# A hybrid decoder layer on one core: four tiles and one norm change place

## The chip, the cores and the metric

The kernel runs on one core of one Trainium2 chip. A core has five engines that run their own instruction queues in order: TensorE (PE) multiplies matrices out of SBUF into PSUM, VectorE (DVE) and ScalarE (ACT) do elementwise work, GpSimd (POOL) does a little of it here, and SyncE (SP) only issues transfers. A transfer is handed to a queue and carried by 16 DMA engines. The metric is the device time of one execution in microseconds (us); of several executions the median counts, and less is better.

## The reference

One decoder layer works on 2048 tokens of 1024 channels in float32.

```
h    = rmsnorm(x, g_mix) * (1 + sc_m) + sh_m
q, k, v, f_logit, u = split(h @ w_in)
attn = rmsnorm(forgetting_attention(q, k, v, log_sigmoid(f_logit + b)), g_attn_out)
ssm  = rmsnorm(s5_ssm(u, ...), g_ssm_out)
x    = x + gt_m * (concat(attn, ssm) @ w_out)
h    = rmsnorm(x, g_ffn) * (1 + sc_f) + sh_f
gate, val = split(h @ w_up)
x    = x + gt_f * ((silu(conv3(gate)) * val) @ w_down)
out  = rmsnorm(x, g_final)
```

The six vectors sh_m, sc_m, gt_m, sh_f, sc_f, gt_f are `silu(c) @ w_ada + b_ada`. The attention has 8 heads of 64; the state space model (ssm) has 32 groups; the middle width of the MLP is 2816 (22 tiles of 128 channels). The last line divides each token by its root mean square, so it needs all 1024 channels of a token before it can scale one of them.

## The kernel before, in words

The tokens are four blocks of 512. Nearly every product is made of three matmuls, because each operand is split into a rounded part and a rest (`_hi` and `_lo`): hi x hi, hi x lo, lo x hi. A weight goes through `w_raw` (two buffers, loaded on SP's queue), ACT makes `w_hi` from it (L77, or L107 where the rest is kept in HBM), and DVE makes `w_lo` (L78). `w_hi` and `w_lo` have three buffers each.

The program is written with tile pools, and a scheduler turns it into one fixed order for each engine, from priorities and from its own estimate of when a tile's memory comes free. Engines then wait for each other by semaphores, but never change that order. The tile pools are stacked: when a pool is closed, the next one is laid over its memory. Pools opened by the helper `opened` ask for their waits tile by tile.

The stages, in the order of time:

1. Projections of all blocks, tables of the ssm, then the ssm itself (pools `ssm` in SBUF and `ssm_ps` in PSUM) beside attention of block 0 (`attention((0,))`) and the q/k/v projections of blocks 2 and 3 (`proj_qkv`, L428, results in `vst`). In the same stage `ada_mid` (L1091) works out gt_f (`mod["tf"]`): per half, eight slices of w_ada arrive in two tiles `wada` (tags `ka3` and `ka4` of the pool `att`), DVE adds them into one accumulator `ada_mid` (L1100, L1102), and PE turns it into a column (`ada_col`, L316). The accumulator lies in the pool `ssm`. Attention holds augmented keys in the tiles `ka0` to `ka2`, taken in a cycle by the heads of block 0; after this stage `ka3`, `ka4` and `kx0` join the cycle, each after a memset on POOL (L1136).
2. The pools `ssm` and `ssm_ps` are closed; over them come `rows`, `ffn` and `act` in SBUF and the PSUM pools `ffn_ps` (three banks `ff_ps`) and `sc_ps`. `mix_t(0)` loads attention and ssm rows of block 0 (L1199, L1200), normalises them, transposes them on PE (L1212) and splits them; `out_proj(0)` multiplies by w_out (L1238); `h2_of` makes the MLP's input. These stand under high priority.
3. `attention((1, 2, 3))` is traced next at normal priority, and its matmuls (L943, L986, L987, L1007, L1011) are spread over the MLP of blocks 0 and 1, which is made in four groups of 6, 6, 5 and 5 channel tiles (`FFG`): `up` (L1264) for each tile of the group, then `down` (L1296 to L1298) for eight output tiles d, added into the tiles `yt`. In the last group of block 0 the next block's `out_proj(1)` and its norm `modulate` (L391, L379, L380) are put in. `finish(0, sq)` then makes the final norm of block 0: `token_sums` on PE (L341), `rsqrt_mean` as a chain of 12 small DVE instructions (L166 to L176), four transposes (L347), a copy on ACT (L367), eight products on DVE (L1311) and eight stores (L1313). It is traced ahead of block 1's `up`.
4. Blocks 2 and 3 share their up product in a Strassen-like form: `up_pair` makes seven products of 12 matmuls (L1387) for each of the 22 tiles. Its first two operands, b11 and b21, lie in tiles of the pool `h` (nine `h_hi`, nine `h_lo`). The results `ah` and `al` go to HBM (L1431).
5. All pools but a few are closed, `h` among them, and a pool `act` is laid over everything. `down_pair(2)` and `down_pair(3)` read the activations back (L1448, 22 tiles of 512 KB) and make the down product (L1480 to L1482): two halves of four d, four PSUM tiles `acc_ps`, the groups one after the other. In the very last group of block 3 (`cut`) each matmul is made for 256 tokens at a time, p = 0 then p = 1, so that `finish_last` (L341, L166 to L176, L347, L1517, L1521 to L1526) can norm and store the first half ahead of the second. The four weights of that group come out of the three buffers `w_hi` and `w_lo`.

Of the kernel before, what the change touches and what calls it, by code (L numbers as in the profile page):

```python
# [12 lines left out]
F32 = mybir.dt.float32  # L13
F32R = mybir.dt.float32r
# [8 lines left out]
P = 128  # L23
# [4 lines left out]
TB = S // NB  # L28
# [83 lines left out]
def hybrid_layer(ctx, tc, x, c_t, w_ada, b_col, gains, w_flat, bf_row, a_re, a_im, log_dt,  # L112
# [978 lines left out]
    def ada_mid(pool, sec, key):  # L1091

        for hf in range(2):
            acc = pool.tile([P, TB], F32, name="ada_mid", tag="ada_mid", bufs=1)
            for k in range(KT):
# [42 lines left out]

    qa_t, ka_all = itertools.cycle(aug_tiles(att_pool, "qa", 2)), aug_tiles(att_pool, "ka", 3)
    ka_t = [itertools.cycle(ka_all)]  # L1140
    att_ps = opened(att_ctx, "att_ps", bufs=1, space=PSUM, side="right")
    with tc.tile_pool(name="ssm", bufs=2) as sp, tc.tile_pool(name="ssm_ps", bufs=1, space=PSUM) as sps:
# [3 lines left out]
        attention((0,))  # L1146
        mid = itertools.chain(*(ada_mid(sp, sec, key) for sec, key in ((5, 'tf'),)))
        for b in (2, 3):
# [20 lines left out]
    yt = []  # L1169
    ka_t.append(itertools.cycle(ka_all + aug_tiles(att_pool, "ka", 2, 3) + aug_tiles(fp, "kx", 1)))  # L1170

# [262 lines left out]
    def down_pair(b, ap, dps, misc, tail):  # L1434
# [9 lines left out]
        def load_act(g):  # L1444
            c0 = sum(FFG[:g])
            for c in range(c0, c0 + FFG[g]):
                t = ap.tile([P, 2, TB], F32R, name="act", tag="act", bufs=NFF)
                Q.dma_start(t.bitcast(F32), act_d[c][b % 2])  # L1448
                act.append(t)

        load_act(0)
        for half in range(2):
# [3 lines left out]
            for g, n in enumerate(FFG):  # L1456
# [9 lines left out]
                for p in range(2 if cut else 1):  # L1466
                    ts = slice(p * 256, (p + 1) * 256) if cut else slice(0, TB)
                    for d in ds:
                        if d not in ws:
                            ws[d] = weights.get(*dn_slots[g][d])  # L1470
                        wh, wl = ws[d]
# [3 lines left out]
                        for c in range(n):  # L1475
                            ah, al = act[c0 + c][:, 0, ts], act[c0 + c][:, 1, ts]
                            a, bb = wh[:, c * P : (c + 1) * P], wl[:, c * P : (c + 1) * P]
# [87 lines left out]
    for b in range(2):  # L1565
        i = 0
        for g, n in enumerate(FFG):
            act = [up(h2, i + c) for c in range(n)]
            i += n
# [24 lines left out]
        if b == 0:  # L1594
            x1 = x1n
            finish(b, sq)
    first = up_pair(0, ops, ups)
# [34 lines left out]


# [78 lines left out]
```

## Time and profile before

| | us |
|---|---|
| median of 3 executions | 2672.63 (2672.21 to 2674.73) |
| the profiled execution | 2669.64 |
| its span | 2667.8 |
| TensorE busy in it | 2571.5 (96%) |
| mean granted TensorE clock | 0.973 |

The profiled execution lasted 2669.64 us, of which the span, from the first to the last instruction, is 2667.8; 1.84 us lie around it. It is 2.99 us below the median. A view by windows gives, for a stretch, its length and then the busy time of each engine with the number of its instructions, the clock that the throttle granted TensorE (1.00 is full speed), the share of the DMA engines' time that was busy, and the rate. A timeline gives start and length in us, the engine, the line of the kernel, and in brackets how long the engine had been idle and what released it. SPq is the issue of a transfer on SyncE's queue, not the transfer. Where matmuls follow each other closely their shown durations overlap, since they are pipelined; their spacing is what they cost.

### The profile page before, as it was taken

To read this page: it belongs to the slowest core of one execution; us is meant where nothing else is said; L and a number is where in the kernel's file an instruction comes from. 1 tells how busy PE (TensorE), PEld (TensorE's weight loads), DVE (VectorE), ACT (ScalarE), POOL (GpSimd) and SP (SyncE) were. 2 spreads that over 40 slices of the span, in tenths; PEclk is the share of its full clock that TensorE was granted. 3 is DMA by queue.
4 is the path that set the end of the run, shared out by engine and by line. 5 is a ranking of instruction groups with operands and counts; after the bars stand their busy time and mean duration, and the time that the engine had idled before them with its cause. 6 is when DMAs were issued, how large, how long until landed. Compare 5 with 4: busy or idle time off the path is not lost. (4 is left out here: it accounts for less than half of the span.)

```text
span 2667.8 us, 35631 instructions
## 1 busy us (share of the span) xinstructions
PE 2571.5 (96%) x12343; PEld 2082.7 (78%) x12343; DVE 1928.8 (72%) x3568; ACT 1240.3 (46%) x2056; POOL 190.4 (7%) x146
## 2 busy tenths in 40 slices
PE   6999999998999999999999999999979999999997
PEld 3889878886788888887788888887858888877886
DVE  7989589967787787887976867655687777762333
ACT  3423255644455545565565645555544444442221
POOL 0001000000000000000000000000043343310000
PEclk8999999998899999999899999999989999999998
DMA  8487986666456555656556555557522323236562
GB/s 316 146 268 222 306 252 202 211 205 209 148 199 224 188 183 171 201 173 204 186 181 203 190 174 194 163 203 262 189 103 97 124 97 121 98 136 239 200 225 93
DMA packets 264196, 500.62 MB, mean 188 GB/s; under 512 B 26928, under 2 KB 111792, under 8 KB 264016
## 3 DMA queue, kind: packets, MB, share of 16 engines
q1 hardware_dynamic: 262192, 493.10, 56.2%
q0 software_dynamic: 1280, 4.20, 0.4%
q8 instruction: 98, 1.61, 0.2%
q10 hardware_dynamic: 544, 1.05, 0.1%
q14 instruction: 82, 0.67, 0.1%
HBM read 371.17 MB, written 127.01 MB: 187 GB/s over the span
## 5 line engine op out<-in xcount | busy, mean ns | idle before, releaser
L78 DVE TENSOR_TENSOR w_lo<-w_raw,w_hi 128x1024 fp32r<-128x1024 f32 (+2 forms) x219 | 235.9, 1079 | 214.6 <-ACT w_hi L77 210.9
L77 ACT CAST w_hi<-w_raw 128x1024 fp32r<-128x1024 f32 (+2 forms) x219 | 203.3, 929 | 363.6 <-PE acc_ps L1481 100.9
L1264 PE MATMUL ff_ps<-h_lo,w_hi 128*128 128x512 f32 x704 | 279.3, 397 | 0.2 <-DVE h_lo L380 0.2
L1264 PE MATMUL ff_ps<-h_hi,w_lo 128*128 128x512 f32 x704 | 279.3, 397 | 0.0
L1264 PE MATMUL ff_ps<-h_hi,w_hi 128*128 128x512 f32 x704 | 279.2, 398 | 0.0
L996 ACT ACTIVATE pf<-sc_ps 128x512 f32<-128x512 f32 (+1 forms) x320 | 168.6, 542 | 165.3 <-PE sc_ps L987 84.6
L948 DVE TENSOR_REDUCE mx<-sc_ps 128x1 f32<-128x512 f32 (+2 forms) x320 | 195.8, 621 | 68.2 <-PE sc_ps L943 38.6
L998 DVE TENSOR_TENSOR pl<-pf,ph 128x512 fp32r<-128x512 f32 (+1 forms) x320 | 195.9, 620 | 29.5 <-ACT ph L997 28.8
L997 ACT CAST ph<-pf 128x512 fp32r<-128x512 f32 (+1 forms) x320 | 178.1, 568 | 81.7 <-PE o_ps L1007 78.4
L1006 DVE TENSOR_TENSOR acc<-acc,pf 128x512 f32<-128x512 f32 (+2 forms) x264 | 159.3, 606 | 22.6 <-ACT pf L996 19.4
L107 ACT CAST w_hi<-w_raw 128x1024 fp32r<-128x1024 f32 (+2 forms) x100 | 96.3, 963 | 142.9 <-PE ff_ps L1264 52.7
L1264 PEld LDWEIGHTS ff_ps<-h_lo,w_hi 128*128 128x128 f32 x704 | 132.9, 189 | 29.5 <-DVE h_lo L380 0.5
L1264 PEld LDWEIGHTS ff_ps<-h_hi,w_hi 128*128 128x128 f32 x704 | 133.1, 189 | 28.6
L1264 PEld LDWEIGHTS ff_ps<-h_hi,w_lo 128*128 128x128 f32 x704 | 132.9, 189 | 28.8
L1480 PE MATMUL acc_ps<-act,w_hi 128*128 128x512 f32 (+1 forms) x372 | 144.5, 389 | 10.6 <-DMA act<-act 6.5
L1481 PE MATMUL acc_ps<-act,w_hi 128*128 128x512 f32 (+1 forms) x372 | 143.9, 387 | 0.0
L1482 PE MATMUL acc_ps<-act,w_lo 128*128 128x512 f32 (+1 forms) x372 | 143.4, 387 | 0.2 <-DVE w_lo L78 0.2
L1296 PE MATMUL ff_ps<-act_hi,w_hi 128*128 128x512 f32 x352 | 140.0, 398 | 0.9 <-ACT rt L367 0.9
L1297 PE MATMUL ff_ps<-act_lo,w_hi 128*128 128x512 f32 x352 | 139.4, 397 | 0.0
L1298 PE MATMUL ff_ps<-act_hi,w_lo 128*128 128x512 f32 x352 | 139.0, 396 | 0.0
L986 PE MATMUL sc_ps<-qb,kb 128*128 128x512 f32 (+2 forms) x320 | 127.8, 400 | 2.3 <-DVE mx L948 1.3
L1007 PE MATMUL o_ps<-ph,vv 128*128 128x512 f32 (+1 forms) x320 | 122.2, 382 | 0.0
(521 smaller groups left out, 6457.5 us busy)
## 6 DMA issues: line engine op xcount, KB each, us to landing
w_raw<-in_w_flat SPq DMA_DIRECT2D x193, 512.0 KB
w_lo<-wlo SPq DMA_DIRECT2D x68, 512.0 KB
wlo<-w_lo SPq DMA_DIRECT2D x52, 512.0 KB
w_raw<-in_w_flat SPq DMA_DIRECT2D x64, 384.0 KB
act<-act SPq DMA_DIRECT2D x44, 512.0 KB
kb<-kb SPq DMA_DIRECT2D x80, 256.0 KB
vv<-v SPq DMA_DIRECT2D x80, 256.0 KB
w_raw<-in_w_flat SPq DMA_DIRECT2D x64, 320.0 KB
```

The costliest lines, as they stand in the source:

```text
L77: nc.scalar.copy(hi[:, :n], raw[:, :n])
L78: nc.vector.tensor_tensor(out=lo[:, :n], in0=raw[:, :n], in1=hi[:, :n].bitcast(F32), op=ALU.subtract)
L948: V.reduce_max(out=mx[:, s, ch : ch + 1], in_=ps[:, 0:n], axis=AX.X)
L996: A.activation(pf[:, cs], ps[:, cs], AF.Exp)
L997: A.copy(ph[:, cs], pf[:, cs])
L998: V.tensor_tensor(out=pl[:, cs], in0=pf[:, cs], in1=ph[:, cs].bitcast(F32), op=ALU.subtract)
L1006: eng.tensor_tensor(out=acc[j][:, cs], in0=acc[j][:, cs], in1=pf[:, cs], op=ALU.add)
L1264: T.matmul(ps, lhsT=lt, rhs=rt, start=(n == 0), stop=(n == 23))
L1296: T.matmul(ps, lhsT=a, rhs=ah[:, ts], start=(c == 0), stop=False)
L1480: T.matmul(pss[d][:, ts], lhsT=a, rhs=ah, start=st, stop=False, skip_group_check=cut)
L1481: T.matmul(pss[d][:, ts], lhsT=a, rhs=al, start=False, stop=False, skip_group_check=cut)
L1482: T.matmul(pss[d][:, ts], lhsT=bb, rhs=ah, start=False, stop=sp_, skip_group_check=cut)
```

## The change

The accumulator of `ada_mid` leaves the pool `ssm` and takes the tag `ka2` of the pool `att`; so attention of block 0 has two key tiles in its cycle (`ka0`, `ka1`), and `ka2` joins later, with `ka3`, `ka4` and `kx0`. The final norm of block 0 is traced inside block 1's first group, after the third of its six `up`. The activations of the first down group of blocks 2 and 3 are read into `h_hi` and `h_lo` (two loads of 256 KB each instead of one of 512 KB), and the pool `h` stays open to the end; the others get a tag of their own. The four weights of the last group are split into tiles of their own (`cut_hi4` to `cut_lo7`).

```diff
     def ada_mid(pool, sec, key):
-            acc = pool.tile([P, TB], F32, name="ada_mid", tag="ada_mid", bufs=1)
+            acc = pool.tile([P, TB], F32, name="ada_mid", tag="ka2", bufs=1)
...
-    qa_t, ka_all = itertools.cycle(aug_tiles(att_pool, "qa", 2)), aug_tiles(att_pool, "ka", 3)
+    qa_t, ka_all = itertools.cycle(aug_tiles(att_pool, "qa", 2)), aug_tiles(att_pool, "ka", 2)
...
-        mid = itertools.chain(*(ada_mid(sp, sec, key) for sec, key in ((5, 'tf'),)))
+        mid = itertools.chain(*(ada_mid(att_pool, sec, key) for sec, key in ((5, 'tf'),)))
...
-    ka_t.append(itertools.cycle(ka_all + aug_tiles(att_pool, "ka", 2, 3) + aug_tiles(fp, "kx", 1)))
+    ka_t.append(itertools.cycle(ka_all + aug_tiles(att_pool, "ka", 3, 2) + aug_tiles(fp, "kx", 1)))
...
         def load_act(g):
-                t = ap.tile([P, 2, TB], F32R, name="act", tag="act", bufs=NFF)
-                Q.dma_start(t.bitcast(F32), act_d[c][b % 2])
-                act.append(t)
+                if g == 0:
+                    act.append(h_parts())
+                    for j, t in enumerate(act[-1]):
+                        Q.dma_start(t.bitcast(F32), act_d[c][b % 2, :, j])
+                else:
+                    t = ap.tile([P, 2, TB], F32R, name="act", tag=f"act{c}", bufs=1)
+                    Q.dma_start(t.bitcast(F32), act_d[c][b % 2])
+                    act.append((t[:, 0], t[:, 1]))
...
                         if d not in ws:
-                            ws[d] = weights.get(*dn_slots[g][d])
+                            so, sn = dn_slots[g][d]
+                            own = [ap.tile([P, sn], F32R, name=f"w_{nm}", tag=f"cut_{nm}{d}", bufs=1)
+                                   for nm in ("hi", "lo")] if cut else (None, None)
+                            ws[d] = weights.split(weights.raw(so, sn), sn, *own)
...
-            act = [up(h2, i + c) for c in range(n)]
+            act = []
+            for c in range(n):
+                act.append(up(h2, i + c))
+                if b == 1 and g == 0 and c == 2:
+                    finish(0, sq0)
...
         if b == 0:
-            x1 = x1n
-            finish(b, sq)
+            x1, sq0 = x1n, sq
...
-    hp_ctx.close()
     with ExitStack() as stk:
...
             down_pair(b, ap, dps, misc, b == 3)
+    hp_ctx.close()
```

More of the change, by code (lines that the diff above doesn't have):

```diff
@@ L1475, in down_pair @@
                         for c in range(n):
-                            ah, al = act[c0 + c][:, 0, ts], act[c0 + c][:, 1, ts]
+                            ah, al = (t[:, ts] for t in act[c0 + c])
                             a, bb = wh[:, c * P : (c + 1) * P], wl[:, c * P : (c + 1) * P]
```

## The prediction

> **What bounds the kernel now.** I read the busy times of the page first, then windows over the whole span, and then the timelines of the engines around each window in which TensorE is short of its length or its clock is below 1.00.
>
> ```profile
> PE 2571.5 (96%) x12343; PEld 2082.7 (78%) x12343; DVE 1928.8 (72%) x3568; ACT 1240.3 (46%) x2056; POOL 190.4 (7%) x146
> ```
>
> ```profile
> 604.00:616.00 12.00, 7.90 (x45) 6.67 (x43) 7.32 (x12) 3.10 (x5) 0.54 (x2) 0.82 0.78 269
> 616.00:636.00 20.00, 15.96 (x52) 11.18 (x53) 13.85 (x45) 7.55 (x18) 0.96 (x2) 0.51 0.64 211
> 636.00:644.00 8.00, 6.28 (x38) 4.72 (x36) 7.85 (x20) 6.47 (x13) 0.00 (x0) 1.00 0.41 131
> 650.00:1250.00 600.00, 598.26 (x2743) 478.47 (x2742) 479.63 (x857) 318.66 (x530) 0.00 (x0) 0.99 0.58 191
> 1279.00:1291.00 12.00, 10.53 (x30) 5.84 (x29) 10.10 (x23) 4.38 (x9) 0.00 (x0) 0.72 0.48 146
> 1306.00:1312.00 6.00, 3.16 (x23) 2.77 (x22) 5.97 (x11) 3.76 (x6) 0.00 (x0) 0.95 0.93 327
> 1312.00:1322.00 10.00, 8.99 (x33) 7.05 (x34) 7.86 (x25) 4.32 (x9) 0.00 (x0) 0.52 0.09 33
> 1322.00:1900.00 578.00, 576.64 (x2608) 465.66 (x2607) 391.06 (x731) 316.04 (x520) 0.00 (x0) 1.00 0.60 200
> ```
>
> TensorE bounds it: 598.26 of 600 us and 576.64 of 578 us in the long stages. So a microsecond that TensorE gets back ahead of such a stage ends the program a microsecond earlier, as long as the same instructions remain. There are two ways to lose one: idle time, and work at a clock of about one half, which follows a place where TensorE had idled. I price the second as busy time x (1 - clock). The change touches four such places.
>
> **Place 1, the accumulator (604 to 644).** Idle time is 4.10 + 4.04 + 1.72 us; the clock costs 7.90 x 0.18 = 1.4 and 15.96 x 0.49 = 7.8. Together 19.1 us are lost here. The instructions around it:
>
> ```profile
> 589.74 0.32 SPq L1044 DMA_DIRECT2D att<-at  x1
> ...
> 617.71 0.33 SPq L1199 DMA_DIRECT2D row<-att  x1
> ```
>
> ```profile
> 616.45 0.52 POOL L1136 MEMSET kx<- 3x512 f32 x1
> ```
>
> ```profile
> 615.98 1.87 PE L316 MATMUL sc_ps<-ones,ada_mid 128*128 128x1 f32 x8 [1.62 <-DVE ada_mid L1102]
> ...
> 628.21 0.80 PE L987 MATMUL sc_ps<-qa,ka 67*128 67x512 f32 x1 [3.82 <-DMA qa<-rrow]
> ...
> 635.99 0.82 PE L1212 MATMUL ff_ps<-ident,row 128*128 128x128 f32 x6
> ...
> 642.46 0.47 PE L1238 MATMUL ff_ps<-yt,w_hi 128*128 128x512 f32 x1
> ```
>
> ```profile
> 614.84 0.42 DVE L489 TENSOR_TENSOR vst<-vq_ps,vst 128x256 fp32r<-128x256 f32 x1
> ```
>
> ```profile
> 592.00:600.00 8.00, 8.00 (x69) 7.91 (x68) 4.59 (x8) 2.91 (x5) 0.00 (x0) 1.00 0.46 157
> ```
>
> The last attention tile of block 0 is stored at 589.74, but its rows are fetched only at 617.71, though `mix_t(0)` has high priority; and kx0, which needs no data, is set at 616.45. Both lie over the memory of the pool `ssm`, and both come with the last reader of `ada_mid` (L316, 615.98). I read this as the scheduler holding the whole pool for that one tile. With the accumulator in `ka2`, the row loads may go at about 592, and squares, rsqrt and scaling follow on ACT and DVE. The next wait is then for PSUM: the `ff_ps` banks lie where `vq_ps` was, whose last reader is the DVE instruction that ends at 615.26. From first transpose to first `out_proj` matmul took 642.46 - 635.99 = 6.5 us, so `out_proj(0)` can start at 621.7 instead of 642.46, and it is 192 matmuls that need no attention result of block 1. They cover the wait of 3.82 for `rrow` and the 1.72 idle after 636: 5.5 us. Of the 15.96 us busy, 5.6 lie ahead of 621.7; the other 10.4 x 0.49 = 5.1 come back but for about 0.7 while the clock recovers: 4.4. Against it stand eight row loads of 256 KB, 2.1 MB, ahead of v stores, weights and `wada` in SP's queue. At the rate of the twelve 512 KB loads quoted under place 3 (6.29 MB in 17.04 us, 369 GB/s) they are 5.7 us of transfer, and 592 to 600 has 8 x 0.54 = 4.3 free. So the v projection is late by 1.4 to 2 us. The other edits here I cost at nothing: with two key tiles in block 0 a head's key load waits for the head before last, as its `qa` load (two tiles) does already; `ka2` is set only after L316, with its load some 5 us later than before, and the second head's maxima that need it give way to `out_proj`. If that cover is gone, it costs those 5. **I take 8.0 us**; bounds -5.7 (all transfer time lands on TensorE, nothing is filled) and 19.1.
>
> **Place 2, the norm of block 0 (1306 to 1322).** Idle 2.84 + 1.01; the clock 8.99 x 0.48 + 3.16 x 0.05 = 4.5; together 8.3 us.
>
> ```profile
> 1306.10 0.39 PE L1298 MATMUL ff_ps<-act_hi,w_lo 128*128 128x512 f32 x1
> ...
> 1309.78 0.66 PE L1042 MATMUL sc_ps<-ident,sums 128*128 128x128 f32 x4 [2.51 <-ACT sums L1039]
> ...
> 1320.25 1.06 PE L347 MATMUL ff_ps<-ident,rs_y 128*128 128x128 f32 x4
> ...
> 1320.96 0.77 PE L1264 MATMUL ff_ps<-h_hi,w_hi 128*128 128x512 f32 x1
> ```
>
> ```profile
> 1302.01 1.42 DVE L380 SCALAR_TENSOR_TENSOR h_lo<-h_f,mod_sf,h_hi 128x512 fp32r<-128x512 f32 x2
> ...
> 1313.85 0.76 DVE L380 SCALAR_TENSOR_TENSOR h_lo<-h_f,mod_sf,h_hi 128x512 fp32r<-128x512 f32 x1
> ...
> 1322.49 5.38 DVE L1311 SCALAR_TENSOR_TENSOR yt<-yt,gain,rt 128x512 f32<-128x512 f32 x8
> ```
>
> The last down matmul of block 0 is at 1306.10, and block 1's `up` begins at 1320.96, right behind the norm's transposes, though four of its eight input tiles are ready by 1303.4 and the last at 1314.6. Without the norm in front, 4 tiles x 3 matmuls x 2 branches = 24 matmuls can run at once; at 576.64 / 2608 = 0.22 us each they last 5.3 us, to 1311.6, by when tiles arrive in twos. The gap of 2.51 is filled, and with it goes the half clock. DVE is busy 5.97 of 6.00 us there, so the late tiles may still be waited for; that is why I keep back 1.8. The norm itself (12 small matmuls, a chain of 12 DVE instructions, the 5.38 us on DVE, eight stores of 256 KB) comes some 30 us later among three further `up`, which are its cover, and ends ahead of the first down that writes `yt`. It holds an `ff_ps` bank twice. If the transposes stand too near to their sums, TensorE waits for the chain, 3.10 us by a row of place 4. **I take 6.5 us**; bounds -3.1 and 8.3.
>
> A rule of the Trainium skill ("TensorE: Matmul & The Clock Gate", section "Part 1: The HAM clock gate (the "warmup" mystery)") says that the clock halves after an idle window of about 3.4 us and returns after about 3.4 us of sustained work. By it the 2.51 us here would not have been enough to halve the clock, and filling it need not bring the clock back; the row of 1312 to 1322 has 0.52 behind it all the same.
>
> **Place 3, from up to down (2387 to 2431).**
>
> ```profile
> 2373.14 0.39 PE L1387 MATMUL up_y<-h_hi,w_lo 128*128 128x512 f32 x1
> ...
> 2393.96 0.76 PE L1480 MATMUL acc_ps<-act,w_hi 128*128 128x512 f32 x1 [6.48 <-DMA act<-act]
> ```
>
> ```profile
> 2380.78 8.68 SPq L69 DMA_DIRECT2D w_raw<-in_w_flat  x3
> 2389.50 17.04 SPq L1448 DMA_DIRECT2D act<-act  x12
> ```
>
> ```profile
> 2371.00:2387.00 16.00, 16.00 (x70) 12.93 (x69) 9.02 (x12) 6.03 (x9) 0.00 (x0) 1.00 0.35 116
> ...
> 2394.00:2397.00 3.00, 3.00 (x8) 2.38 (x9) 1.22 (x1) 1.04 (x1) 0.00 (x0) 0.54 0.90 333
> ...
> 2425.00:2431.00 6.00, 6.00 (x15) 4.35 (x15) 2.37 (x3) 1.34 (x2) 0.00 (x0) 0.51 0.72 218
> ```
>
> ```profile
> PE acc_ps L1480 <- ACT w_hi L77: 3.6, 1, 3.6
> ```
>
> ```profile
> 2396.33 7.76 DMA act<-al
> ```
>
> TensorE waits 6.48 us for the first activation, whose load is issued at 2389.50, when the pools are closed. In the `h` tiles it need not wait for that: b11 and b21 are read for the last time at 2373.14, and up to 2387 the DMA engines are 65% free, 10 us, while 3.1 MB take 8.5. So the first down matmul follows the last up matmul: 6.48 + 3.00 x 0.46 = 7.9 us. A second wait, 3.6 us for a weight queued behind the activations, with 6.00 x 0.49 = 2.9 of clock, I leave as it is: 3.1 MB less are in the queue, but TensorE also comes 6.5 us sooner. If it goes too, the gain is 14.4. The other way: the next group's tiles lie over `rows`, which the store of `al` leaves only at 2404.1, and a load took 4.5 us from 2389.50 to its matmul, so 2408.6; four d of 18 matmuls at 0.22 us end at 2403.4. That would be a new wait of 5.2 with 2.9 of clock, -0.2 in all. The store's 7.76 us stand behind twelve loads that will be gone, so **I take 7.9 us**, by the row of the 6.48 us wait; bounds -0.2 and 14.4. Block 3's loads into `h` are covered by a full TensorE.
>
> **Place 4, the end.**
>
> ```profile
> 2650.70 0.50 PE L341 MATMUL misc_ps<-ones,sq_acc 128*128 128x1 f32 x4
> 2654.30 0.45 PE L347 MATMUL misc_ps<-ident,rs_y 128*128 128x128 f32 x1 [3.10 <-DVE rs_y L176]
> ...
> 2660.11 0.66 PE L347 MATMUL misc_ps<-ident,rs_y 128*128 128x128 f32 x2 [4.40 <-DVE rs_y L176]
> ```
>
> ```profile
> 2642.74 0.73 ACT L77 CAST w_hi<-w_raw 128x640 fp32r<-128x640 f32 x1 [0.20 <-PE acc_ps L1481]
> ```
>
> ```profile
> 2651.90 0.42 DVE L333 TENSOR_TENSOR sq_acc<-sq_acc,sq 128x256 f32<-128x256 f32 x1
> ...
> 2661.29 2.05 DVE L1524 SCALAR_TENSOR_TENSOR yt<-yt,gain,misc_ps 128x256 f32<-128x256 f32 x5 [1.33 <-ACT rt L1517]
> ```
>
> The fourth weight is split at 2642.74, when a buffer is released by the first weight's second half; so the first half's sums come at 2650.70, after all 120 matmuls, and the second half's norm queues behind the first's on PE (3.10) and on DVE (4.40). With four buffers of its own the first half is complete after 60 of the 120 matmuls, and its norm runs beside the other 60. The second half's squares are ready at 2651.90 + 0.42 = 2652.3, as now. Sums of 0.50 and an undisturbed chain of 3.10 give 2655.9; then, as now, 2661.29 - 2660.11 = 1.2 to the first product, so 2657.1 instead of 2661.29. **I take 4.2 us**; bounds 1 (the two chains still meet on DVE) and 6 (the squares are earlier too, by the waits that the present order puts between the matmuls).
>
> **Sum.** 8.0 + 6.5 + 7.9 + 4.2 = 26.6 us. The profiled execution took 2669.64, so 2643.0; it lies 2.99 below the median 2672.63, and the sum carried to the median is 2646.0.
>
> **The rivals.** (A) Place 1 pays nothing: `opened` asks for waits by tile, so something else may order the rows, or transfers and `rrow` take the place of the wait: 2654.0. For it speaks a DMA share of 0.78 from 604 to 616. (B) Place 3's wait turns up one group later, as worked out: 2654.1. (C) The waits that I left go too, 13.6 (the two later windows of place 1), 8.3, 14.4 and 6 us: 2630.3. (D) The idle time of place 2 goes but the half clock has another cause and stays, 4.5 us: 2650.5; the page named above speaks for it, the row of 0.52 against it. (E) The change does not do what it says: the scheduler's order stays the same in the first three places and only the end pays: 2668.4, no change that can be measured. (F) Slower: the new order loses the cover elsewhere. From 1279 to 1291 attention's DVE work already starves TensorE, 1.47 idle and 10.53 x 0.28 = 2.9 of clock, 4.4 us. Blocks 1 to 3 have 24 heads; from seven more such places the gain is gone, and at eight more the time is 2646.0 + 35.2 = 2681.2. Against it: in 1200 us of that stage this is the one large place.
>
> **How the numbers follow.** The forecast has 0.42, A 0.17, B 0.12, C 0.08, D 0.08, E 0.07, F 0.06. A difference below 0.2%, 5.3 us, is about what a measurement of this kernel cannot tell from none. So faster 0.87, same 0.07 (E), slower 0.06 (F). The range goes from C, 2630, to 2663, where A and B come together (2662.1); it leaves out E and F, 0.13, and some of the edges. The likeliest time is 2646.0.
>
> **What would show it.** Place 1: `row<-att` issued near 593, and L1238 beginning near 622. Place 2: L1264 of block 1 right behind the last L1298, and the clock at 1.00 through it. Place 3: no wait of L1480 for `act`, its loads ahead of the last up matmul. Place 4: L77 of the last weight ahead of the first L341, and the wait of 4.40 of the last L347 about as short as the 3.10 of the one before. I would be wrong if TensorE's idle time moved to another window instead of leaving, above all next to transfers at 590 to 610 and 2400 to 2425.

## The result, and the profile after

The changed kernel takes 2659.72 us (median of 4 executions, 2654.97 to 2661.21) against 2673.24 us for the kernel before on the same chip (4 executions, 2672.21 to 2674.73). The ratio is 0.9946, with a 95% interval of 0.9929 to 0.9963: 13.5 us less, between 10 and 19. Repeated later it was 2657.83 us, ratio 0.9944 (0.9932 to 0.9956). The forecast was 2646.0, a gain of 26.6 us. The time lies inside the range of 2630 to 2663, the sign was right, and about half of the gain was there.

To see where it went, I counted TensorE's lost time: in rows of 5 us of the view by windows, (5 - busy) + busy x (1 - clock), summed over each stretch. This is the pricing of the prediction, applied to the whole span. One column is one profiled execution; the kernels of the later columns are explained under the experiments.

```
us lost              before norm   h    cut   no    acc  | after again load load  mix  late load  all
                            alone alone alone acc   alone|                  +tail            +late
0 to 575              55.5  57.9  59.7  59.8  62.8  59.6 | 62.7  59.3  57.4  60.4  55.7  56.8  57.1  59.3
575 to 725 (place 1)  27.2  26.0  27.9  26.8  24.8  22.9 | 19.7  22.1  21.0  20.4  19.3  14.0  17.1  16.6
725 to 1225            0.0   0.2   0.2   0.1   0.5   0.0 |  0.0   0.0   0.0   0.0   0.0   0.9   0.9   0.5
1225 to 1400 (pl. 2)  13.2   8.2  13.1  14.0   7.0  17.8 |  6.5   6.2   4.8  11.3   6.3   8.1   9.0  10.9
  of it 1225 to 1275   0.0   0.0   0.0   0.0   0.0   0.0 |  1.7   0.0   0.0   0.0   0.0   4.0   5.5   5.3
  of it 1275 to 1300   4.7   4.8   4.4   4.3   3.4  10.7 |  0.0   0.0   0.0   0.0   0.0   0.0   0.0   0.0
  of it 1300 to 1400   8.5   3.4   8.7   9.7   3.6   7.1 |  4.8   6.2   4.8  11.3   6.2   4.1   3.6   5.6
1775 to 1850           1.4   1.4   1.4   1.4   1.4   1.2 |  0.1   0.1   0.6   0.1   0.1   0.1   0.1   0.2
1850 to 1990          19.5  20.2  20.0  20.6  20.6  18.0 | 24.5  23.3  24.2  22.1  23.1  22.6  25.2  23.1
2350 to 2600 (pl. 3)  14.7  15.4   8.6  15.2   8.0  13.9 |  9.2   8.6   4.1   2.8   8.7   9.5   4.4   3.1
2600 to the end (4)   16.2  15.5  16.1  13.0  13.2  15.6 | 13.5  13.3  13.0  13.7  13.5  13.6  13.5  13.6
```

(Nothing is lost between 1400 and 1775 and between 1990 and 2350 in any of them. The span less the lost time is 2520.0 in the profile before and 2519.2 to 2525.4 in the others, so the count closes within about 6 us and not better.)

The first row is no effect of the change. The kernels "norm", "h", "cut" and "no acc" have, up to 575 us, the same order of instructions on PE, DVE, ACT and SP as the kernel before, and still read 57.9 to 62.8; the kernel before reads 55.5. The kernels with the order of the change read 55.7 to 62.7 there. So the 7.2 us between the profile before and the profile after are no more than what chance gives; the profile before happens to be the lowest of all. The places have to be read one by one.

**Place 1.** The timeline of the kernel after, SP's queue and then PE:

```profile
575.97 0.54 SPq L1199 DMA_DIRECT2D row<-att  x1
...
588.26 0.47 SPq L934 DMA_DIRECT2D kx<-kb  x1
...
613.82 0.32 SPq L1044 DMA_DIRECT2D att<-at  x1
615.92 0.32 SPq L1199 DMA_DIRECT2D row<-att  x1
```

```profile
619.37 3.54 PE L1212 MATMUL ff_ps<-ident,row 128*128 128x128 f32 x16 [1.04 <-DVE vst L489]
628.16 1.09 PE L347 MATMUL ff_ps<-ident,rs_y 128*128 128x128 f32 x4 [5.26 <-DVE rs_y L176]
628.90 0.78 PE L1238 MATMUL ff_ps<-yt,w_hi 128*128 128x512 f32 x1
```

The first of the four attention rows is fetched at 575.97, before block 0's attention is complete, so the pool's wait for `ada_mid` is gone, as the prediction read it. (With the accumulator alone moved it is fetched at 574.63; with the rest of the change and the accumulator in `ssm` at 624.60, again just behind L316.) `out_proj(0)` starts at 628.90 instead of 642.46, and the wait of 3.82 for `rrow` is gone from this place. But the last attention tile is now stored at 613.82 (589.74 before), while the keys of a head of block 1 (`kx`) are already fetched at 588.26, and PE then waits 5.26 us for the norm of the attention rows. Before, the load of `kx` stood at 623.00:

```profile
623.00 0.45 SPq L934 DMA_DIRECT2D kx<-kb  x1
```

Smaller waits in the kernel after remain where block 1's heads start:

```profile
678.12 0.50 PE L943 MATMUL sc_ps<-ka,qa 66*128 66x512 f32 x1 [1.05 <-DVE mx L948]
...
686.26 0.80 PE L987 MATMUL sc_ps<-qa,ka 67*128 67x512 f32 x1 [0.86 <-DMA qa<-rrow]
```

**Place 2.** PE's timeline (the last down matmul of block 0, block 1's up, the norm), and then the windows from the last wait on (length, busy time of PE, PEld, DVE, ACT and POOL, clock, DMA share, GB/s):

```profile
1277.45 0.39 PE L1298 MATMUL ff_ps<-act_hi,w_lo 128*128 128x512 f32 x1
1278.50 0.39 PE L1264 MATMUL ff_ps<-h_hi,w_hi 128*128 128x512 f32 x1
...
1306.99 0.50 PE L1264 MATMUL ff_ps<-h_hi,w_lo 128*128 128x512 f32 x1 [1.12 <-DMA w_lo<-wlo]
```

```profile
1327.28 0.95 PE L341 MATMUL ff_ps<-ones,sq_acc 128*128 128x1 f32 x8
...
1339.95 0.65 PE L347 MATMUL ff_ps<-ident,rs_y 128*128 128x128 f32 x4 [0.17 <-DVE rs_y L176]
```

```profile
1310.00:1328.00 18.00, 18.00 (x87) 14.75 (x85) 13.72 (x28) 9.81 (x17) 0.00 (x0) 1.00 0.67 228
1328.00:1336.00 8.00, 6.24 (x22) 3.14 (x21) 8.00 (x17) 5.21 (x9) 0.00 (x0) 1.00 0.53 181
1336.00:1341.00 5.00, 4.66 (x16) 2.99 (x16) 4.08 (x16) 1.19 (x3) 0.00 (x0) 0.66 0.18 53
```

Up follows down at once. The norm's sums stand at 1327.28 and its transposes at 1339.95, 12.7 us later, and the wait of 0.17 in front of these is all that is left of its chain. The wait of 2.51 and the half clock behind it are gone. A smaller gap, 1.76 us of 8, is new beside DVE at 8.00 of 8, and so is the wait of 1.12 for `w_lo`. The last down matmul of block 0 stands 29 us earlier than before (1277.45 and 1306.10), so the same stretch of time does not hold the same work in the two profiles.

**Place 3.** SP's queue, and PE's longest wait:

```profile
2374.96 0.32 SPq L1450 DMA_DIRECT2D h_lo<-act  x1
...
2378.08 18.21 SPq L69 DMA_DIRECT2D w_raw<-in_w_flat  x4
2396.34 8.33 SPq L1453 DMA_DIRECT2D act<-act  x11
2405.68 1.62 SPq L69 DMA_DIRECT2D w_raw<-in_w_flat  x2
```

```profile
2417.22 0.80 PE L1488 MATMUL acc_ps<-act,w_hi 128*128 128x512 f32 x1 [5.25 <-ACT w_hi L77]
```

The wait of 6.48 for `act` is gone: the last of the loads into `h_hi` and `h_lo` is issued at 2374.96, ahead of the last up matmul. A wait of 5.25 for a `w_hi` comes at 2417; two weights are issued at 2405.68, behind eleven loads of 512 KB. It is the wait of 3.6 of before, at the same matmul, the 109th of the down product in both profiles. The row of before:

```profile
2424.65 0.80 PE L1480 MATMUL acc_ps<-act,w_hi 128*128 128x512 f32 x1 [3.55 <-ACT w_hi L77]
```

**Place 4.** PE and DVE:

```profile
2640.03 0.50 PE L341 MATMUL misc_ps<-ones,sq_acc 128*128 128x1 f32 x4
2644.68 0.40 PE L347 MATMUL misc_ps<-ident,rs_y 128*128 128x128 f32 x2 [0.93 <-DVE rs_y L176]
2645.33 0.58 PE L341 MATMUL misc_ps<-ones,sq_acc 128*128 128x1 f32 x4 [0.24 <-DVE sq_acc L333]
2650.28 0.66 PE L347 MATMUL misc_ps<-ident,rs_y 128*128 128x128 f32 x2 [4.37 <-DVE rs_y L176]
```

```profile
2627.43 0.73 ACT L77 CAST w_hi<-w_raw 128x640 fp32r<-128x640 f32 x1 [2.80 <-DMA w_raw<-in_w_flat]
```

The last weight is split at 2627.43, ahead of the first half's sums, and the first half's norm runs beside matmuls: its wait fell from 3.10 to 0.93. The last wait stayed: 4.37 after 4.40.

**A loss that the prediction had given no place.** Between 1850 and 1990 TensorE loses about 3 us more. The rows of the kernel after, with the row of before for the same DVE instruction (the last attention tile of block 3) in a fence of its own:

```profile
1785.11 0.69 DVE L1043 TENSOR_TENSOR at<-at,sc_ps 128x512 f32<-128x512 f32 x1 [0.44 <-PE sc_ps L1042]
```

```profile
1837.44 0.69 DVE L1043 TENSOR_TENSOR at<-at,sc_ps 128x512 f32<-128x512 f32 x1 [0.60 <-PE sc_ps L1042]
```

```profile
1855.86 1.24 PE L1212 MATMUL up_y<-ident,row 128*128 128x128 f32 x8 [0.73 <-ACT h_f L1214]
...
1865.70 0.50 PE L1238 MATMUL ff_ps<-hh,w_hi 128*128 128x512 f32 x1 [1.45 <-DVE hh L377]
```

The last attention tile comes 52 us later. `mix_t(3)` needs it, and its transposes and first matmuls now wait for ACT and DVE; before, they had no such wait.

### The profile page after: what moved, and what is told of

It reads as the page before. It is cut to its first block, busy times and chain, and to the rows that moved or that the text cites. A ratio compares the mean times of both kernels' runs of the same rounds, so it can differ in the third digit from the quotient of the medians.

```text
span 2658.3 us, 35609 instructions
## 1 busy us (share of the span) xinstructions
PE 2559.9 (96%) x12343; PEld 2072.1 (78%) x12343; DVE 1928.9 (73%) x3568; ACT 1241.8 (47%) x2056; POOL 190.6 (7%) x146
## 3 DMA queue, kind: packets, MB, share of 16 engines
q10 hardware_dynamic: 544, 1.05, 0.1%
## 5 line engine op out<-in xcount | busy, mean ns | idle before, releaser
L1387 PE MATMUL up_x<-hh,w_hi 128*128 128x512 f32 x352 | 113.4, 401 | 6.8 <-DVE hh L377 5.1
L1011 PE MATMUL o_ps<-pl,vv 128*128 128x512 f32 (+2 forms) x312 | 116.9, 377 | 1.4 <-DVE pl L998 1.3
L1387 PE MATMUL up_z<-hh,w_hi 128*128 128x512 f32 x352 | 112.0, 399 | 1.4 <-ACT vz L1403 1.4
```

Source lines behind the costliest of these rows:

```text
L1387: mark[0] = T.matmul(ps, lhsT=lt, rhs=rt, start=(first and n == 0), stop=(n == 11), skip_group_check=not first)
```

## The experiments

**1. The four parts, each alone on the kernel before** (columns acc, norm, h and cut). Their edits are the hunks of the change: the first four for the accumulator, the two in the block loop for the norm, `load_act` with the moved `hp_ctx.close()` for the h tiles, the `own` buffers for the last weights.

```diff
-            acc = pool.tile([P, TB], F32, name="ada_mid", tag="ada_mid", bufs=1)
+            acc = pool.tile([P, TB], F32, name="ada_mid", tag="ka2", bufs=1)
```

> Only the accumulator is moved (first part of the change, alone on the kernel before). Theory 1, the edit pays at its own place: lost TensorE time between 575 and 715 us falls from 26.9 to 19.7 as in the profile after (7.2 less), the waits for qa<-rrow of 3.82 and 1.31 and the half clock behind 695 are gone, a wait of about 5.3 for rs_y in front of out_proj(0) is new; the 3.3 us that the profile after loses more between 325 and 575 come with it, so the run is 3.9 us faster than before. Theory 2, the reordering costs elsewhere: the loss of 5.0 at 1855 to 1870 comes with this edit too, then it is 1.1 us slower. Theory 3: all of the early loss (0 to 575, 7.2 us) belongs to this edit, then the gain is nothing or less at every run.

```diff
+                if b == 1 and g == 0 and c == 2:
+                    finish(0, sq0)
```

> Only the norm of block 0 is moved into block 1's up (second part, alone on the kernel before). Theory 1: lost time between 1250 and 1400 falls from 13.2 to 6.5, and the loss at 1855 to 1870 belongs to another edit: 6.7 us faster. Theory 2: the new order behind 1300 brings the 5.0 us of 1855 to 1870: 1.7 us faster. In both, the instructions ahead of about 1290 us stand in the order of before, so that the lost time up to there is that of before but for what differs between executions; a difference of some us there says how much of the early 3.9 us is no effect of code.

```diff
+                if g == 0:
+                    act.append(h_parts())
```

> Only the first activations of down go into the h tiles (third part, alone on the kernel before). Theory 1: it pays here what it paid in the whole change, 14.7 to 8.8 us lost between 2350 and 2500, so 5.9 us faster, with the wait of 6.48 for act gone and a wait of about 5.2 for a w_hi one group later. Theory 2, by the step of the prediction: the second wait stays at 3.6 us, 7.9 us faster.

```diff
+                            own = [ap.tile([P, sn], F32R, name=f"w_{nm}", tag=f"cut_{nm}{d}", bufs=1)
+                                   for nm in ("hi", "lo")] if cut else (None, None)
```

> Only the last four weights get buffers of their own (fourth part, alone on the kernel before). Theory 1: the last two norm chains still meet, last wait for rs_y stays 4.4 us, end 2.8 us earlier as the lost time behind 2600 reads in the profile after (16.2 to 13.5). Theory 2, by the prediction: 4.2 us faster. The first half's norm then runs beside the second half's 60 matmuls, so L77 of the last weight stands ahead of the first L341 in both.

Measured, 11 executions each, against 33 of before (median 2672.67): accumulator 2670.35, ratio 0.9991 (0.9981 to 1.0); norm 2669.23, 0.9990 (0.9981 to 0.9998); h tiles 2668.72, 0.9987 (0.9978 to 0.9995); own buffers 2671.15, 0.9994 (0.9983 to 1.0004). As ratios of 2672.67 these are 2.4, 2.7, 3.5 and 1.6 us, 10.2 together. Each interval is some 2.5 us wide to either side, so the lost time of the table has to decide between the theories. (For the norm and the h tiles the place shows more, 5.2 and 6.2 us, than the upper ends of their intervals, 5.1 and 5.9.)

The accumulator alone wins 3.6 at its place (22.9 against 26.5, the mean of the five kernels that have it in `ssm`) and loses 4.4 at place 2 (17.8 against 13.4), where attention's waits grow around the norm of block 0. These are rows of PE of this run:

```profile
1281.56 0.51 PE L943 MATMUL sc_ps<-ka,qa 66*128 66x512 f32 x1 [1.29 <-DVE mx L948]
...
1297.65 0.80 PE L987 MATMUL sc_ps<-qa,ka 67*128 67x512 f32 x1 [1.40 <-DMA qa<-rrow]
```

Theory 1 had its place at 19.7, and theory 2 named the wrong place for the loss: 1850 to 1990 is 18.0 in it, no worse than before. Theory 3 falls with the 59.6 of the first row. The norm alone wins 5.2 at place 2 and loses nothing at 1855; that is theory 1 by the profile, though the time, 2.7 us, is nearer to theory 2's 1.7. The loss at 1855 comes with neither of them alone. For the h tiles and the own buffers theory 1 holds by the places: 14.8 to 8.6, with a wait of 5.47 for `w_hi` at that 109th matmul, and 15.8 to 13.0.

**2. The changed kernel again** (column again). Nothing is edited.

> The changed kernel itself, once more. Lost TensorE time (idle plus busy x (1 - clock)) between 0 and 575 us was 55.5 in the profile before, 62.7 in the profile after, and 57.9, 59.7 and 59.8 in the runs of parts two, three and four, whose instructions stand there in the order of before. Theory 1, chance: this profile reads between 55 and 60 there. Theory 2, the new order costs there: again above 61. In both, 1850 to 1990 again reads 24 to 25 (19.5 to 20.6 in the other four), since that loss is a matter of order; 575 to 750 about 19.7. Time 2658 to 2661.

2657.83 us, ratio 0.9944 (0.9932 to 0.9956). Up to 575 it lost 59.3: theory 1, chance. 1850 to 1990 is 23.3 and place 1 is 22.1, so single profiles differ by 1 to 3 us at one place too.

**3. The change without the accumulator's part** (column no acc). The tag `ada_mid`, the pool `sp` and three key tiles are put back; the rest stays.

```diff
-            acc = pool.tile([P, TB], F32, name="ada_mid", tag="ka2", bufs=1)
+            acc = pool.tile([P, TB], F32, name="ada_mid", tag="ada_mid", bufs=1)
```

> The change without its first part: norm, h tiles and buffers of the last weights, the accumulator where it was. Theory 1, the accumulator pays 7.4 us at its place and 1.7 at place 2 and costs 4.5 at the tail of attention (1855 to 1870): 575 to 750 reads 27 lost, 1250 to 1400 8.2, 1850 to 1990 20, 2350 to 2500 8.7, behind 2600 13.2; 4.6 us slower than the whole change, so about 2664. Theory 2, the four parts add up as they did alone (2.3, 3.4, 4.0 and 1.5 us): 2.3 slower than the whole change. Theory 3, the new order of attention costs what the place gives: the same time as the whole change, 2660.

2661.53 us, ratio 0.9953 (0.9941 to 0.9965). That is 2.4 us above the changed kernel's 0.9944, as theory 2 had it; the intervals overlap, so neither 4.6 nor nothing is excluded. By the table the pieces are those of theory 1 but smaller: the accumulator in `ka2` wins 3.6 at place 1 (24.8 against 21.2, the mean of the five kernels with it and the same order there) and 1.2 at 1810, and loses 2.9 at 1850 to 1990 (20.6 against 23.5, the mean of the four kernels with the change's order there). In this run the last attention tile is at 1797, not at 1837:

```profile
1797.20 0.69 DVE L1043 TENSOR_TENSOR at<-at,sc_ps 128x512 f32<-128x512 f32 x1 [0.44 <-PE sc_ps L1042]
```

With the accumulator alone that tile is at 1821.86, with the norm alone at 1794.75. So most of the delay of attention's end comes with the accumulator's part, and the loss at 1855 comes only where both parts are in. Of the 3.6 that the accumulator wins at its place, 2.9 are given back there.

**4. Place 3: loads of the next group, two per weight** (column load), on the changed kernel, as all that follow. `load_act` gets a first and a last tile.

```diff
-                        if half == 0 and d == ds[1] and not last:
+                        if half == 0 and d > ds[0] and not last:
                             with tc.issue_after(weights.last.ins):
-                                load_act(g + 1)
+                                load_act(g + 1, 2 * (d - 1), 2 * d)
```

> The changed kernel, but the activations of down's next group are loaded two with each of the second, third and fourth weight of the group instead of all with the second. Theory 1, the wait of 5.25 for w_hi at 2417 is the wait of two weights behind eleven activations in SP's queue: it goes, and with it the half clock behind it; lost between 2350 and 2500 falls from 8.8 to about 2, the run is 6 us faster than the changed kernel. Theory 2, the transfers as such are too many for the time (4.6 MB in a group of 72 matmuls, 16 us): the wait turns up as waits for act instead, and the time stays within 2 us.

2654.68 us, ratio 0.9930 (0.9917 to 0.9943). SP's queue and the wait that is left, of this run (in the view of waits: us over the span, number, longest):

```profile
2390.48 3.90 SPq L1453 DMA_DIRECT2D act<-act  x8
2394.97 0.33 SPq L69 DMA_DIRECT2D w_raw<-in_w_flat  x1
2396.25 1.57 SPq L1453 DMA_DIRECT2D act<-act  x2
```

```profile
PE acc_ps L1488 <- ACT w_hi L77: 1.9, 1, 1.9
```

The weights no longer stand behind eleven loads, the wait falls from 5.25 to 1.9, and place 3 from 8.6 to 4.1 (2.8, 4.4 and 3.1 in the three later kernels with the same loads). Theory 1: the wait was two weights behind activations in one queue, not a limit of the transfers.

**5. Place 1: the state space half of out_proj(0) ahead of the transposes** (column mix). `mix_t(0)` hands back its attention part as a function, and `out_proj(0)` calls it after half of its first two outputs.

```diff
+        if b == 0:
+            for d in range(2):
+                half(d, (4, 5, 6, 7))
+            mt["att"]()
+            half(2, (4, 5, 6, 7))
```

> The changed kernel, but out_proj(0) runs the state space half of its first two outputs (24 matmuls) ahead of the transposes that wait 5.26 us for rs_y, and of the third behind them. Theory 1, that wait is what is left of place 1 and the 24 matmuls fill it: the wait goes, lost between 610 and 640 falls from 10.1 to 3 or less, the run is 5 to 7 us faster than the changed kernel. Theory 2, the attention rows behind the transposes (four DVE instructions of 0.7 and the splits) are late next: a wait of about 2.5 for them takes its place, 2 to 4 us faster. Theory 3, key tiles or row loads are late again and nothing is gained.

2657.66 us, ratio 0.9944 (0.9930 to 0.9959): the same as the changed kernel. The wait of 5.26 is gone, and theory 2's wait took its place, without the 2 to 4 us that theory 2 had expected. PE, then DVE:

```profile
630.10 0.96 PE L1247 MATMUL ff_ps<-yt,w_hi 128*128 128x512 f32 x3 [2.82 <-ACT yt L376]
```

```profile
627.98 0.75 DVE L1102 SCALAR_TENSOR_TENSOR ada_mid<-wada,sil,ada_mid 128x512 f32<-128x512 f32 x1 [1.50 <-DMA wada<-in_w_ada]
628.65 2.73 DVE L1220 SCALAR_TENSOR_TENSOR row<-row,gain,rt 128x512 f32<-128x512 f32 x4
```

The scaling of the attention rows (L1220, L1219 without the edit) stands on DVE behind steps of the accumulator that wait for transfers of `wada`, the last one for 1.50.

**6. Place 1: the accumulator's second half behind those rows** (column late).

```diff
-            proj_qkv(b, h, qs_ps, each=mid)
+            proj_qkv(b, h, qs_ps, each=mid if b == 2 else iter(()))
...
+    with tc.issue_after(vm0.ins):
+        for _ in mid:
+            pass
```

`vm0` is the last scaling of `mix_t(0)`; the line that adds `ka2` to `ka4` and `kx0` to the cycle moves behind this block.

> The changed kernel, but the second half of the accumulator (eight loads of wada and its eight DVE instructions) is queued on DVE behind the scaling of the attention rows of block 0, instead of among the norm chain in front of out_proj(0). Theory 1, the chain of rs_y is late in the changed kernel since DVE waits in order for wada's transfers (0.63 and 1.23 at 626 and 629 in the profile after): the wait of 5.26 falls to 3 or less and lost between 575 and 750 falls from 20 to 22 (profile after, its repetition) to 17 to 19. Theory 2, the chain itself (twelve instructions after the last attention sums) is the wait: it stays about 5. Theory 3, the accumulator's end is late instead and holds the keys of block 1 at 676 to 690: what is won ahead is lost there.

2654.65 us, ratio 0.9935 (0.9923 to 0.9948), which overlaps the changed kernel's 0.9944; the profile has to decide. In the kernel after the norm chain runs like this on DVE:

```profile
620.89 0.17 DVE L166 TENSOR_SCALAR rs_v<-ss_att 128x4 f32<-128x4 f32 x1
...
625.76 0.75 DVE L1102 SCALAR_TENSOR_TENSOR ada_mid<-wada,sil,ada_mid 128x512 f32<-128x512 f32 x1 [0.63 <-DMA wada<-in_w_ada]
626.43 0.15 DVE L175 SCALAR_TENSOR_TENSOR rs_t<-rs_t,rs_v 128x4 f32<-128x4 f32 x1
...
627.86 0.15 DVE L176 SCALAR_TENSOR_TENSOR rs_y<-rs_t,rs_y 128x4 f32<-128x4 f32 x1
```

From first to last it is 7.1 us, with three steps of the accumulator and four splits (L377) between. Without the accumulator (a fence of this experiment) it is 3.6, from 616.33 to 619.92, with two such splits between:

```profile
616.33 0.16 DVE L166 TENSOR_SCALAR rs_v<-ss_att 128x4 f32<-128x4 f32 x1
...
619.76 0.16 DVE L176 SCALAR_TENSOR_TENSOR rs_y<-rs_t,rs_y 128x4 f32<-128x4 f32 x1
```

```profile
620.07 0.62 PE L347 MATMUL ff_ps<-ident,rs_y 128*128 128x128 f32 x4 [1.37 <-DVE rs_y L176]
```

PE's wait for it falls to 1.37 and place 1 to 14.0 (17.1 in a second kernel with the same order). At the place that is theory 1. Theory 3's loss is not at 676 to 690, but experiment 8 finds it elsewhere.

**7. Place 4: the first half's products behind the second half's chain** (column load+tail). The loads are those of experiment 4. A third PSUM tile `misc_ps` keeps the held products from holding up anything.

```diff
         r = rsqrt_mean(ps[:, 0:2], 2, D)
+        if p == 1:
+            with tc.issue_after(chain[0].ins):
+                while held:
+                    held.pop(0)()
```

> The kernel with the spread loads of activations (b3_load), and in the last norm the first half's four products on DVE (1.66 us) stand behind the second half's chain of twelve instead of ahead of it, with a third misc bank so that they hold up nothing. Theory 1, place 4 was priced too high because the two chains still meet on DVE: the last wait for rs_y falls from 4.37 to about 3.1, lost behind 2600 falls from 13.2 to 12. Theory 2, the chain is slowed by something else (its second and third instruction took 0.40 and 0.65 us in the profile after, beside POOL's products of the first half, and 0.17 elsewhere): the four products go but the wait shrinks by less than 0.5. The time is that of b3_load less 1, which the runs can't tell; the profile decides. Lost between 2350 and 2500 again about 4.

2652.22 us, ratio 0.9925 (0.9912 to 0.9939). The last wait only fell to 3.96 and the end did not get shorter (13.7). PE, DVE and POOL in this run, where the lines of the helpers are two higher:

```profile
2641.36 0.66 PE L349 MATMUL misc_ps<-ident,rs_y 128*128 128x128 f32 x2 [3.96 <-DVE rs_y L178]
```

```profile
2637.84 0.65 DVE L171 TENSOR_SCALAR rs_i<-rs_i 128x2 int32<-128x2 int32 x1
2638.52 0.64 DVE L176 TENSOR_TENSOR rs_t<-rs_i 128x2 f32<-128x2 f32 x1
2639.19 0.65 DVE L177 SCALAR_TENSOR_TENSOR rs_t<-rs_t,rs_v 128x2 f32<-128x2 f32 x1
2639.87 0.16 DVE L178 SCALAR_TENSOR_TENSOR rs_y<-rs_t,rs_i 128x2 f32<-128x2 f32 x1
```

```profile
2637.06 2.76 POOL L1548 TENSOR_TENSOR yt<-yt,rt 128x256 f32<-128x256 f32 x4 [286.32 <-ACT rt L1533]
```

While POOL multiplies the first half (2637.06 to 2639.82), three instructions of the chain take 0.65 instead of 0.16; when it ends, they take 0.16 again. Theory 2; the kernel of experiment 8 with everything shows the same wait of 3.96. No run leaves POOL out there, so that this shortens the end is not shown.

**8. Everything together (column all), and the two edits that won most at their place (column late+load).** The edits are those of experiments 4 to 7, and of 4 and 6:

```diff
+                                load_act(g + 1, 2 * (d - 1), 2 * d)
...
+            mt["att"]()
...
+    with tc.issue_after(vm0.ins):
...
+            with tc.issue_after(chain[0].ins):
```

> Everything together on the changed kernel: the state space half of out_proj(0) first (b4_mix), the second half of the accumulator late (c2_late), spread loads and the late products of the last norm (c1_loadtail). Theory 1, the gains stand at different places and add up: lost 575 to 750 about 15 to 17, 2350 to 2500 about 4, behind 2600 about 12, and 2650 us or less. Theory 2, a new order of attention takes back at 1250 to 1400 or 1850 to 1990 what the places give, as in the run of the accumulator alone (17.8 at 1250 to 1400): 2654 or more.

2655.31 us, ratio 0.9930 (0.9918 to 0.9943).

```diff
+                                load_act(g + 1, 2 * (d - 1), 2 * d)
...
+    with tc.issue_after(vm0.ins):
```

> The changed kernel with the two edits that took something away by the profile: spread loads of activations (b3_load) and the second half of the accumulator behind the attention rows on DVE (c2_late), without the other order of out_proj(0) and of the last norm. Theory 1, the gains add: lost 575 to 750 about 18, 2350 to 2500 about 3 to 4, a mean near 2650, 8 us under the changed kernel's 2658.7. Theory 2, past place 3 nothing more shows in the time, since the new order of attention takes as much elsewhere: the same as the spread loads alone, 2653 to 2655.

2651.74 us, ratio 0.9923 (0.9908 to 0.9937), where the kernel before took 2669.49.

In the first, theory 2. In the second the interval takes in both theories; the ratio stands nearer to theory 2. The places keep their gains (place 1 at 16.6 and 17.1, place 3 at 3.1 and 4.4), but the time is that of the spread loads alone. The rows of place 2 show where some of it goes. From 1225 to 1275 the three kernels with the late half lose 4.0 (late), 5.5 (late+load) and 5.3 (all), and all others 0.0 to 1.7: TensorE, busy for all 50 us there in the kernel after, is busy for 47.2 to 47.5, and waits mostly for parts of attention that DVE makes, as in experiment 6 for `pl`, the rest part of attention's exponentials:

```profile
1245.70 0.58 PE L1011 MATMUL o_ps<-pl,vv 128*128 128x512 f32 x1 [1.73 <-DVE pl L998]
```

So the 4 to 7 us that the late half wins in front of `out_proj(0)` are for the most part lost again 600 us later, by the order that comes with it. From 1300 on, single profiles differ much without any edit there: that row reads 4.8 and 11.3 in two kernels with one order on PE there, experiments 4 and 7. A row of each:

```profile
1301.37 0.50 PE L1264 MATMUL ff_ps<-h_hi,w_lo 128*128 128x512 f32 x1 [1.07 <-DMA w_lo<-wlo]
```

```profile
1303.56 0.80 PE L1266 MATMUL ff_ps<-h_hi,w_lo 128*128 128x512 f32 x1 [2.56 <-DMA w_lo<-wlo]
```

The same transfer is waited for 1.07 in the one and 2.56 in the other, where the granted clock is 0.53 from 1305 to 1310.

The four kernels with spread loads have ratios of 0.9923 to 0.9930, all others 0.9935 or more. The version to keep is experiment 4: clearly below the kernel before, and by the ratios some 4 us below the changed one. Its own interval still overlaps that of the changed kernel; the four kernels together and place 3 in their profiles carry that second claim.

## Why the prediction was half right

By the table the places give 18.1 us, from means over kernels with the same order at a place: 26.5 to 21.2 at place 1, 13.4 to 7.2 at place 2, 1.4 to 0.2 at 1810, 14.8 to 8.6 at place 3, 15.8 to 13.3 at place 4, and 20.2 to 23.5 between 1850 and 1990. The executions say 13.5 and 15.0, with intervals up to 19 and 18. The rest of 3 to 5 us is not settled; it is not more than what single profiles differ by, and not more than the count closes to.

**What bounds it, and the clock.** Right. The stretches 1400 to 1775 and 1990 to 2350 lose nothing before or after, and most of what was won ahead of them shows in the time.

**Place 1, forecast 8.0, measured 5.3.** The cause was read rightly: the pool's wait for one tile held the rows, and with the tile elsewhere the first is fetched 42 us earlier. In the window that was priced the number came near, 7.6 from 610 to 645 (17.6 to 10.0), but not by the path described: `out_proj(0)` starts at 628.90, not at 621.7, behind a new wait of 5.26. And 2.3 are lost again on either side (0.5 to 2.2 from 575 to 610, 8.4 to 9.0 from 645 to 725). The step that failed is "the row loads may go at about 592, and squares, rsqrt and scaling follow on ACT and DVE". It kept the rest of the order as it was. The new order also moved the thing that the rows wait for, attention's last tile, by 24 us, and it put the accumulator's steps, which wait for `wada`, into the norm's chain on DVE. Of a changed place I had listed who waits on PE and not what stands in DVE's queue in front of it; experiment 6 shows that as the price at the place, 4 to 7 us of lost time (21.2 to 17.1 and 14.0), though its own order loses most of them again from 1225 to 1275. Rival A ("something else may order the rows") named part of this, at 0.17, without the mechanism; that the place pays nothing did not come. No row gives the 0.7 us that the forecast set down for the recovery of the clock; in the profile after the clock costs 3.3 from 615 to 635, behind the new wait.

**"The other edits here I cost at nothing".** Wrong, but not for the key loads of block 1: PE waits 1.05 for maxima and 0.86 for `rrow` at 678 and 686, and this is inside the 21.2. The price is at 1855: 3.3 us, where attention of blocks 1 to 3 ends 40 to 52 us later than without the accumulator's part or without the change. Rival F had the idea, the cover lost elsewhere, but priced it as seven and more places like 1279 to 1291 and as the reason for a slower kernel; one place at the end was the case. Why the scheduler's order stretches attention in this way is not shown; every kernel with the accumulator in `ka2` also has only two key tiles for block 0, so the two are not told apart.

**Place 2, forecast 6.5, measured 6.2.** The steps came: up starts at once, the clock stays at 1.00 to 1328, the norm's chain is covered, and part of what is left stands beside a full DVE, for which 1.8 had been kept back. That the number came too is in part luck. Of the 6.2, 4.0 are the loss of 1279 to 1291, ahead of the last down matmul, which the prediction left as it was: 4.5 from 1225 to 1300 in the kernels with the order of before (4.7, 4.4 and 4.3), 0.4 in those with the order of the change. It stays with the norm's part alone (4.8) and without the accumulator's (3.4), so the order that the accumulator's part brings removed it. (The 10.7 of the accumulator alone from 1275 to 1300 lie behind its last down matmul, at 1276.66.) From 1300 on, the whole change wins 2.2 (9.0 to 6.8, its profiles at 4.8 to 11.3), with the gap of 1.76 and a new wait for `w_lo` of 0.95 to 2.56. The norm's part without the accumulator's wins 5.5 there (9.0 to 3.4 and 3.6), near the forecast, and loses nothing from 1300 to 1345. Rival D fell with that: the clock came back with the gap. A rule of the Trainium skill ("TensorE: Matmul & The Clock Gate", section "Part 1: The HAM clock gate (the "warmup" mystery)") spoke for D with its idle window of about 3.4 us; the trace disagrees here too, for behind 1.76 us of idle time between 1328 and 1336 the clock is 0.66.

**Place 3, forecast 7.9, measured 6.2.** The mechanism is right and the term is mis-sized: "a second wait, 3.6 us for a weight queued behind the activations, I leave as it is" grew to 5.25. TensorE comes to that matmul 9.1 us sooner (2411.97 and 2421.10), its weight is split only 7.4 sooner (2417.17 and 2424.60), and the 1.7 between them are what is missing. Rival B's new wait, 5.2 for the next group's first tile at about 2403, did not come: TensorE waits 0.88 for `act` at 2403.10. That the weight is waited for 5.25 is the same number by chance. Experiment 4 takes most of it away by the order of loads alone.

**Place 4, forecast 4.2, measured 2.5.** The step "an undisturbed chain of 3.10" failed: the wait stayed at 4.37. The bound of 1 us had the right idea, that the two halves still meet, but not in their two chains. The second chain meets the first half's products: four of them stand on DVE ahead of it (1.66 us), and without these (experiment 7) the wait is still 3.96, with three instructions of the chain 0.5 us longer each beside POOL's products.

## What to carry to other kernels

Where a scheduler lays down the order, a tile that is moved to lift one wait changes the order far beyond it: list for the new place what stands in front of the awaited instruction on every in-order engine, above all steps that wait for transfers, and look at where the next stage needs the engine that is shared. In a queue of transfers, put small loads that something waits for ahead of bulk that nothing waits for yet. And a change of half a per cent is read by places, with several profiles of kernels that share an order, since one profile differed from another by up to 7 us in a stretch whose order was the same. Where a new order moves the work in time, look at what a stretch holds before a gain in it is put down to one edit: here 4 of the 6 us at the norm's place belonged to another.

## What the runs showed of the hardware

A tiny DVE instruction of 0.16 us took 0.65 while POOL was multiplying tiles of 256 columns, 0.72 us each, four of them in 2.76. The three such instructions of experiment 7 end at 2638.49, 2639.16 and 2639.84, and the POOL products beside them at 2638.46, 2639.14 and 2639.82: each ended within 0.03 us of a product. In the profile before the chain has one such instruction too (L174, 0.65 from 2658.34 on, beside L1522 on POOL). One that ran beside the first product of experiment 7 and read PSUM (`rs_v<-misc_ps`) took 0.16. The Trainium skill ("SBUF — State Buffer", section "Who interferes with whom") says that a DVE instruction with two SBUF inputs contends with a GpSimd instruction that reads SBUF, and that the contention is an exclusive lock. For the two later instructions quoted in experiment 7 (L176, L177) the trace agrees, 0.64 and 0.65 beside 0.72. For the first (L171), which reads one tile, the page asks for a faster mode of DVE, and no run here shows whether it was in one.
